# Seven half-size products instead of eight in the first feed-forward net of a decoder layer too, with its right factors made during the first block's downs

## The chip, the core and the metric

The kernel runs on one core of a Trainium2 chip. The metric is the device time of one launch in microseconds; before the change the median of 3 runs is 1263.14 us (1262.64 to 1269.46). TensorE is called PE, VectorE DVE, ScalarE ACT, GpSimd POOL and SyncE SP, as in the profile.

## What is computed

One inference step of a decoder layer over 544 tokens (512 of a prompt, 8 x 4 new ones of samples with a paged cache), width 1024, hidden width 2816, all in float32. Cut to what matters here:

```
def swiglu(x, w_gate, w_up, w_down):
    return (jax.nn.silu(x @ w_gate) * (x @ w_up)) @ w_down

x = x + 0.5 * swiglu(rmsnorm(x, ffn1_norm), ffn1_w_gate, ffn1_w_up, ffn1_w_down)
h = rmsnorm(x, mix_norm)           # mixer: gated convolution and sparse attention
x = x + concat(y_conv, attn) @ w_out
x = x + 0.5 * swiglu(rmsnorm(x, ffn2_norm), ffn2_w_gate, ffn2_w_up, ffn2_w_down)
```

## The kernel before

**Layout.** The 544 tokens lie along the free dimension, in two halves of 272; the 1024 channels are 8 chunks `c` of 128 partitions, the 2816 features 22 tiles `f` of 128. Each float32 operand is split into a high part (ACT copies it to float32r) and a low part (DVE subtracts), and each product is three matmuls: high by high, high by low, low by high. The weights' parts are `whi` and `wlo` (line 169 and 174, tiles of 128x1024, three slots of each), those of the activations `xh` and `xl`, those of the hidden layer `hh` and `hl`.

**A feed-forward net** runs in blocks of features, `BLOCKS` (line 27), of 8, 8 and 6. For each feature tile of a block the gate `G` and the up `U` are made (48 matmuls of 272 columns each in the plain form, `wmm`, line 194), scaled by the tokens' norm `R`, passed through Silu and multiplied. Then come the downs: for each of the 8 chunks one product `Y` of the block's hidden tiles, which DVE adds to `x` with factor one half. PSUM has eight banks: two places of two banks (`wunit`, tag w), two of one bank (`funit`, tag f), and one each of `sunit` and `tunit`.

**The first net** (`ffn`, line 266) has the plain form throughout. Its beginning (`begin_units`) makes feature 0 while the input still comes in; after the last block each chunk of `x` is squared and split for the mixer (`done1`).

**The second net** (`ffn_late`, line 449) makes features 0 to 3 in the plain form and then two features at once by seven half-size products for eight (Winograd's form of Strassen's). `right` (line 382) makes seven right factors, sums and differences of the quarters of the scaled `x`, kept in `x3h`, `x3l` and in the places of `xh`, `xl`. `factors` (line 343) makes the seven left ones of two weight tiles: POOL makes four sums and differences (`s12`, `s34`, line 367), ACT and DVE their parts (lines 359 and 360). `unit` (line 418) runs the products, each 12 matmuls of 272 columns, 84 in all, and puts them together: ACT copies products 0 and 1 out of PSUM (`m1`, `m5`, lines 436 and 437), DVE adds the others (lines 439 to 447). Products 2 and 4 have the two halves of one two-bank place, products 5 and 6 those of another.

**What sets the order.** A scheduler with a model of the times places each engine's instructions; each engine then runs its own in that order and waits for semaphores. A new tile in a place waits until all readers of the old one are done, and a write into a tile waits for earlier reads of that tile, also of another part of it. Weights come over SP's queue through three buffers `wst` (a fourth, `wst4`, in the second net). POOL's queue also issues the gathers of the cache.

Of the kernel before, what the change touches and what calls it, by code (L numbers as in the profile page):

```python
# [26 lines left out]
BLOCKS = [(0, 8), (8, 16), (16, 22)]  # L27
# [31 lines left out]
SB = 1  # L59
ZB = 1  # L60
# [60 lines left out]
class Trunk:  # L121
# [144 lines left out]
    def ffn(self, wg, wu, wd, done, late=False):  # L266
        nc = self.nc
        wdv = wd.rearrange("(f p) n -> p f n", p=128)

        def hidden(f, G, U):  # L270

            t, s, u = (fp.tile([128, T], F32, name=n, tag=n, bufs=2) for n in ("t", "ts", "u"))

            def scale(dst, src):
                if isinstance(src, list):
                    for cs, p in src:
                        nc.vector.tensor_mul(dst[:, cs], p, self.R[:, cs])  # L277
                else:
                    nc.vector.tensor_mul(dst.rearrange("p (a b) -> p a b", a=2), src[:, :, :HT], self.R.rearrange("p (a b) -> p a b", a=2))  # L279
            scale(t, G)  # L280
            nc.scalar.activation(s, t, AF.Silu)
            scale(u, U)
            nc.vector.tensor_mul(u, u, s)
            nc.scalar.activation(hh[:, f - f0, :], u, AF.Copy)
            nc.vector.tensor_sub(hl[:, f - f0, :], u, hh[:, f - f0, :].bitcast(F32))

        with self.tc.tile_pool(name="ffn", bufs=1) as fp:
            for f0, f1 in BLOCKS:
                nf = f1 - f0
                hh = fp.tile([128, 8, T], F32R, name="hh", tag="hh", bufs=1)  # L290
                hl = fp.tile([128, 8, T], F32R, name="hl", tag="hl", bufs=1)
                for f in range(f0, f1):
                    act = self.xh, self.xl
                    if f == 0 and not late:
                        first = self.begin_units()
                        continue
                    gp = self.cols(wg, f * 128, 128)
                    if f == 1:
                        self.spread()
                        G = list(self.fmm("G", gp, act, KC))  # L300
                        hidden(0, *first)
                    else:
                        G = self.wunit("G")
                        self.wmm(G, gp, act)
                    if f == 0:
                        self.rms_from_S()
                    U = self.wunit("U")
                    self.wmm(U, self.cols(wu, f * 128, 128), act)
                    if f == 0:
                        first = G, U  # L310
                    else:
                        hidden(f, G, U)
                    if f == 2 and not late:
                        self.begin_rest()
                end = f1 == BLOCKS[-1][1]
                for c in range(KC):
                    parts = self.stream(lambda stv: [(stv, wdv[:, f0:f1, c * 128:(c + 1) * 128])], nf, 128)
                    if end and c == KC - 1:
                        for i, (c0, c1) in enumerate(TILES):
                            Y = self.wunit("Y")  # L320
                            self.wmm(Y, parts, (hh, hl), TILES, (i,))
                            if late and i == 0:
                                done(c - 1)
                            xc = self.x[:, c, c0:c1]
                            nc.vector.scalar_tensor_tensor(xc, Y[:, i, :c1 - c0], 0.5, xc, op0=ALU.mult, op1=ALU.add)
                            done(c, i)
                    else:
                        Y = self.wunit("Y")
                        self.wmm(Y, parts, (hh, hl))
                        if end and late and c:  # L330
                            done(c - 1)
                        xc = self.x[:, c, :].rearrange("p (a b) -> p a b", a=2)
                        nc.vector.scalar_tensor_tensor(xc, Y[:, :, :HT], 0.5, xc, op0=ALU.mult, op1=ALU.add)  # L333
                        if end and not late:
                            done(c)

# [36 lines left out]
    def right(self, scale, place, nk):  # L373
# [6 lines left out]
        for k0 in range(0, n, nk):  # L380
            v = fp.tile([128, 2, nk, 2, HT], F32, name="xn", tag=place, bufs=1)
            both = [slice(k, k + 2) for k in range(0, nk, 2)]
            (b11, b12), (b21, b22) = [[v[:, r, :, c] for c in range(2)] for r in range(2)]

            def row(r):
                for k in range(nk):
                    c, dst = r * n + k0 + k, v[:, r, k].rearrange("p c n -> p (c n)")
                    if r == 0:
                        V.scalar_tensor_tensor(dst, self.x[:, c, :], scale[:, c:c + 1], self.R, op0=ALU.mult, op1=ALU.mult)
                    else:  # L390
# [1332 lines left out]
```

## Time and profile before

| | |
|---|---|
| median of 3 runs (lowest, highest) | 1263.14 us (1262.64, 1269.46) |
| the profiled execution's own time | 1267.7 us |
| its span, first to last instruction | 1265.9 us |
| PE busy | 1213.1 us, 96% |
| DVE, ACT, POOL busy | 752.9, 504.0, 347.4 us (59, 40, 27%) |
| mean granted clock of PE | 0.991 of full speed |
| chain of work that ended last, by engine | PE 77%, DVE 15%, issue 3%, DMA 2% |
| the three largest lines of that chain | PE Y L194 20%, PE U L194 11%, PE G L194 10% |

The shares are means over stages with different limits. By the chain and the stage table below, the first net takes the span to 412.3 us, the mixer to about 869 us, and the second net the rest. L194 is the plain form, L433 the seven products, L133 and L137 are the mixer's matmuls and transposes.

### The profile page before, as it was taken

The page shows a single profiled execution, that of the slowest core. Times are in us where ns is not written, and L with a number is a line of the kernel's source. Part 1 is how long each engine was busy: PE and PEld are TensorE (multiplying, and loading weights), DVE is VectorE, ACT ScalarE, POOL GpSimd, SP SyncE. Part 2 cuts the span into 40 slices and gives each one's busy share as a digit, 9 for nine tenths or more (in the row PEclk, how much of TensorE's full clock was granted, in tenths as well). Part 3 has the DMA queues.
Part 4 walks back from the last instruction along what each step waited for, and adds up shares of the span by engine and source line. Part 5 has one row for each costly group of instructions (what it writes and reads, how often), then busy time and mean ns, then how long its engine had stood idle before and what let it go on. Part 6 is the DMA issues. An engine that isn't in the chain of part 4 may idle for free.

```text
span 1265.9 us, 22810 instructions
## 1 busy us (share of the span) xinstructions
PE 1213.1 (96%) x9413; PEld 1093.1 (86%) x9413; DVE 752.9 (59%) x1332; ACT 504.0 (40%) x769; POOL 347.4 (27%) x401
## 2 busy tenths in 40 slices
PE   9999999999999999899988989989989999999998
PEld 8999999999999746776667545779989999999998
DVE  5444334433446216999998853236997469845972
ACT  6322122211324464456534545435544144423432
POOL 3200000000000555665422322321661255305500
PEclk9999999999999998999998999999999999999999
DMA  7432233233222554145222644444314312332322
GB/s 230 127 93 84 84 93 91 84 92 93 84 68 76 163 178 122 51 142 170 68 65 92 201 151 134 155 135 121 91 51 117 114 54 84 112 106 67 96 79 80
DMA packets 184363, 136.09 MB, mean 108 GB/s; under 512 B 5706, under 2 KB 172434, under 8 KB 184260
## 3 DMA queue, kind: packets, MB, share of 16 engines
q1 hardware_dynamic: 171700, 91.62, 24.9%
q0 software_dynamic: 11904, 42.26, 10.4%
q8 instruction: 74, 1.21, 0.4%
q10 hardware_dynamic: 656, 0.76, 0.2%
q14 instruction: 29, 0.24, 0.1%
HBM read 131.66 MB, written 2.96 MB: 106 GB/s over the span
## 4 chain that ended last, share of the span: by engine, by line
PE 77%; DVE 15%; issue 3%; DMA 2%; ACT 1%; POOL 1%; DVEq 0%; ACTq 0%; POOLq 0%
PE Y L194 20%; PE U L194 11%; PE G L194 10%; PE U L433 7%; PE G L433 5%; PE Yo L133 4%; DVE flip L1034 3%; PE KTp L137 2%; PE lg L133 2%; PE nat L133 2%; PE O L133 1%; DMA ckn<-in_cache_k,ik 1%; PE ssc L133 1%; PE gc L133 1%; PE plg L133 1%
## 5 line engine op out<-in xcount | busy, mean ns | idle before, releaser
L169 ACT ACTIVATE whi<-wst 128x1024 fp32r<-128x1024 f32 (+3 forms) x137 | 134.0, 982 | 377.6 <-PE Y L194 123.9
L174 DVE TENSOR_TENSOR wlo<-wst,whi 128x1024 fp32r<-128x1024 f32 (+3 forms) x120 | 138.7, 1156 | 23.8 <-ACT whi L169 21.2
L172 POOL TENSOR_TENSOR wlo<-wst,whi 128x1024 fp32r<-128x1024 f32 (+2 forms) x17 | 34.4, 2022 | 423.8 <-ACT whi L169 423.3
L194 PE MATMUL Y<-hh,whi 128*128 128x272 f32 (+2 forms) x704 | 147.8, 289 | 0.0
L194 PE MATMUL Y<-hh,wlo 128*128 128x272 f32 (+2 forms) x704 | 147.1, 288 | 0.0
L194 PE MATMUL Y<-hl,whi 128*128 128x272 f32 (+2 forms) x704 | 147.0, 288 | 0.0
L194 PEld LDWEIGHTS Y<-hl,whi 128*128 128x128 f32 x704 | 111.3, 189 | 0.0
L194 PEld LDWEIGHTS Y<-hh,whi 128*128 128x128 f32 x704 | 111.0, 188 | 0.0
L194 PEld LDWEIGHTS Y<-hh,wlo 128*128 128x128 f32 x704 | 110.8, 188 | 0.0
L367 POOL TENSOR_TENSOR s<-wst 128x512 f32<-128x512 f32 x36 | 55.6, 1547 | 169.9 <-DMA wst<-in_ffn_w_gate 90.8
L194 PE MATMUL U<-xh,whi 128*128 128x272 f32 x336 | 69.4, 287 | 1.8 <-DVE t L277 1.8
L194 PE MATMUL U<-xh,wlo 128*128 128x272 f32 x336 | 69.1, 288 | 0.0
L194 PE MATMUL U<-xl,whi 128*128 128x272 f32 x336 | 69.0, 287 | 0.0
L194 PE MATMUL G<-xh,whi 128*128 128x272 f32 x320 | 66.1, 288 | 0.0
L194 PE MATMUL G<-xh,wlo 128*128 128x272 f32 x320 | 65.8, 288 | 0.0
L194 PE MATMUL G<-xl,whi 128*128 128x272 f32 x320 | 65.7, 287 | 0.0
L279 DVE TENSOR_TENSOR u<-U,R 128x544 f32<-128x544 f32 x21 | 15.2, 725 | 79.4 <-PE U L194 79.4
L360 DVE TENSOR_TENSOR wlo<-s,whi 128x1024 fp32r<-128x1024 f32 x36 | 55.6, 1544 | 5.9 <-ACT whi L359 5.9
L333 DVE SCALAR_TENSOR_TENSOR x<-Y,x 128x544 f32<-128x544 f32 x23 | 16.7, 725 | 70.8 <-PE Y L194 70.8
L537 DVE SCALAR_TENSOR_TENSOR x<-Y,x 128x544 f32<-128x544 f32 x23 | 16.6, 723 | 65.1 <-PE Y L194 65.1
L194 PEld LDWEIGHTS U<-xh,whi 128*128 128x128 f32 x336 | 52.3, 188 | 2.0 <-ACT whi L169 2.0
L359 ACT ACTIVATE whi<-s 128x1024 fp32r<-128x1024 f32 x36 | 38.0, 1056 | 37.9 <-PE Y L194 19.8
(422 smaller groups left out, 3501.3 us busy)
## 6 DMA issues: line engine op xcount, KB each, us to landing
wst<-in_ffn_w_up SPq DMA_DIRECT2D x44, 512.0 KB, 3.7
wst<-in_ffn_w_gate SPq DMA_DIRECT2D x43, 512.0 KB, 3.6
wst<-in_ffn_w_down SPq DMA_DIRECT2D x32, 512.0 KB, 4.0
wst<-in_w_in SPq DMA_DIRECT2D x16, 512.0 KB, 4.0
wst<-in_ffn_w_down SPq DMA_DIRECT2D x16, 384.0 KB, 3.5
xn<-in_x_prompt SPq DMA_DIRECT2D x4, 512.0 KB
wst<-in_w_in SPq DMA_DIRECT2D x8, 256.0 KB, 7.9
wst<-in_w_out SPq DMA_DIRECT2D x8, 256.0 KB, 2.8
```

The costliest lines, as they stand in the source:

```text
L133: ins = self.nc.tensor.matmul(*args, **kw)
L137: ins = self.nc.tensor.transpose(*args)
L169: nc.scalar.activation(hi, st, AF.Copy)
L172: nc.gpsimd.tensor_tensor(lo, st, hi.bitcast(F32), op=ALU.subtract)
L174: nc.vector.tensor_sub(lo, st, hi.bitcast(F32))
L194: self.nc.tensor.matmul(unit[:, i, :c1 - c0], a[:, k, :], b[:, k, c0:c1], start=k == 0 and j == 0, stop=k == n - 1 and j == 2)
L333: nc.vector.scalar_tensor_tensor(xc, Y[:, :, :HT], 0.5, xc, op0=ALU.mult, op1=ALU.add)
L359: nc.scalar.activation(hi, src, AF.Copy)
L360: nc.vector.tensor_sub(lo, src, hi.bitcast(F32))
L367: nc.gpsimd.tensor_tensor(dst, a, b, op=op)
L433: nc.tensor.matmul(out, w[:, k, :], b[:, k, :], start=k == 0 and j == 0, stop=k == nk - 1 and j == 2)
L1034: V.tensor_scalar(junk, src, cand[:, k:k + 1], None, op0=ALU.is_ge, op1=ALU.add, accum_out=cnt[:, k:k + 1])
```

## The change

The old `ffn` goes, and `ffn_late` becomes `ffn` for both nets. In the first net the blocks are now features 0 to 5, 6 to 13 and 14 to 21. The first block keeps the plain form (its hidden parts are now made for two features at once, `parts_of`); the other two have the seven products. The right factors of the first net are made while the first block's downs run: `right` is now a generator in steps, of which two are taken ahead of each chunk, the chunks come in the order 0, 1, 4, 5, 2, 3, 6, 7, so that no chunk of `x` is updated before it has been read, and with `alone` set POOL has no part in them: DVE scales all eight chunks and makes the differences. In the second net `right` is taken at one go, with POOL, as before. In `unit` product 2 has the place `sunit` and product 4 one of the two `funit`, in both nets; only products 5 and 6 share a two-bank place. At the start the input tiles lie in places that the first net uses later.

```diff
-BLOCKS = [(0, 8), (8, 16), (16, 22)]
+BLOCKS = [[(0, 6), (6, 14), (14, 22)], [(0, 8), (8, 16), (16, 22)]]
+RSTEPS = 2
...
-    def ffn(self, wg, wu, wd, done, late=False):
...
+    def parts_of(self, u, k, hh, hl):
+        if hh is None:
+            hh, hl = (self.fp.tile([128, 8, T], F32R, name=n, tag=n, bufs=1) for n in ("hh", "hl"))
+        self.nc.scalar.activation(hh[:, k:k + 2], u, AF.Copy)
+        self.nc.vector.tensor_sub(hl[:, k:k + 2], u, hh[:, k:k + 2].bitcast(F32))
+        return hh, hl
...
-    def right(self, scale, place, nk):
+    def right(self, scale, place):
...
-                    if r == 0:
+                    if r == 0 or self.alone:
                         V.scalar_tensor_tensor(dst, self.x[:, c, :], scale[:, c:c + 1], self.R, op0=ALU.mult, op1=ALU.mult)
                     else:
                         nc.scalar.activation(dst, self.x[:, c, :], AF.Copy, scale=scale[:, c:c + 1])
...
+                hi, lo = (a[:, j, k0:k0 + 2] for a in t)
+                nc.scalar.activation(hi, src, AF.Copy)
+                V.tensor_sub(lo, src, hi.bitcast(F32))
+            less = (V if self.alone else P).tensor_tensor
             row(0)
             split(0, b11)
+            yield
             row(1)
+            yield
+            less(t3, b22, b12, op=ALU.subtract)
+            V.tensor_sub(b12, b12, b11)
             split(1, b12)
+            yield
+            less(b11, b22, b12, op=ALU.subtract)
             split(2, b11)
+            yield
             split(3, b21)
+            yield
             split(4, t3)
+            yield
+            less(b21, b21, b11, op=ALU.subtract)
             split(5, b22)
+            yield
             split(6, b21)
+            yield
...
         nc.scalar.activation(m1, product(0, self.funit(name)[:, :HT]), AF.Copy)
         nc.scalar.activation(m5, product(1, self.funit(name)[:, :HT]), AF.Copy)
-        w = self.wunit(name)
-        V.tensor_add(z[:, 0], product(2, w[:, 0, :HT]), m1)
+        V.tensor_add(z[:, 0], product(2, self.sunit(name)[:, :HT]), m1)
         p = product(3, self.tunit(name)[:, :HT])
         V.tensor_add(z[:, 3], p, m1)
-        V.tensor_add(z[:, 2], product(4, w[:, 1, :HT]), z[:, 0])
+        V.tensor_add(z[:, 2], product(4, self.funit(name)[:, :HT]), z[:, 0])
...
-    def ffn_late(self, wg, wu, wd, done):
+    def ffn(self, wg, wu, wd, scale, done, late=False):
...
+        def shared(k0):
+            s, u = quarters("s"), quarters("u")
+            return [t[:, 0:4].rearrange("p (k c) n -> p k c n", k=2) for t in (s, u)], s[:, 4:6]
...
+            if f0 == 0 and not late:
+                rest = self.right(scale, shared)
+            for c in (0, 1, 4, 5, 2, 3, 6, 7) if f0 == 0 else range(KC):
+                if f0 == 0:
+                    for _ in range(RSTEPS):
+                        next(rest, None)
+                if c == KC - 1:
+                    list(rest)
                 parts = self.stream(lambda stv: [(stv, wdv[:, f0:f1, c * 128:(c + 1) * 128])], nf, 128)
...
-            xn = [ip.tile([128, D], F32, name=f"xn{t}") for t in range(5)]
+            xn = [xin[:, t] for t in range(4)] + [xin2[:, 0]]
```

Where the scheduler now puts things, at three places. In the first block's downs of the first net, DVE before, from the last up of the block on (`wlo` is the low part of the next weights):

```order
L279 TENSOR_TENSOR u<-U,R 128x544
L283 TENSOR_TENSOR u<-u,ts 128x544
L174 TENSOR_TENSOR wlo<-wst,whi 128x1024
L285 TENSOR_TENSOR hl<-u,hh 128x544
L333 SCALAR_TENSOR_TENSOR x<-Y,x 128x544
L174 TENSOR_TENSOR wlo<-wst,whi 128x1024
L333 SCALAR_TENSOR_TENSOR x<-Y,x 128x544
```

and DVE now, from the second addition on (`s` and `u` hold the scaled quarters; L336 are the factors' low parts, L349 and L356 differences):

```order
L509 SCALAR_TENSOR_TENSOR x<-Y,x 128x544
L336 TENSOR_TENSOR xl<-u,xh 128x544 x2
L336 TENSOR_TENSOR xl<-s,xh 128x544
L349 TENSOR_TENSOR s<-u,s 128x2x272
L175 TENSOR_TENSOR wlo<-wst,whi 128x768
L336 TENSOR_TENSOR x3l<-s,x3h 128x544
L509 SCALAR_TENSOR_TENSOR x<-Y,x 128x544
L356 TENSOR_TENSOR u<-u,s 128x2x272
L175 TENSOR_TENSOR wlo<-wst,whi 128x768
L336 TENSOR_TENSOR x3l<-s,x3h 128x544
L336 TENSOR_TENSOR xl<-u,xh 128x544
L509 SCALAR_TENSOR_TENSOR x<-Y,x 128x544
```

Between two additions, where one weight part stood, there are now three to five instructions more. In the first net, POOL before, from the gathers' addresses on:

```order
L724 TENSOR_SCALAR ik<-pbase 128x8 x4
L900 DMA kn<-in_cache_idx_k,ii 128x1024 x2
L172 TENSOR_TENSOR wlo<-wst,whi 128x984
L1523 MEMSET qbd 128x256
L900 DMA kn<-in_cache_idx_k,ii 128x1024 x3
```

and POOL now, the first of 64 sums and differences of the weights (`s` with its number, four to a unit):

```order
L700 TENSOR_SCALAR ik<-pbase 128x8 x4
L876 DMA kn<-in_cache_idx_k,ii 128x1024 x2
L297 TENSOR_TENSOR s_1408<-wst 128x512
L297 TENSOR_TENSOR s_1409<-wst 128x512
L297 TENSOR_TENSOR s_1408<-s_1408,wst 128x512
L297 TENSOR_TENSOR s_1409<-wst,s_1408 128x512
```

All 64 stand between the second gather and the weight part `wlo` of 128x984; three memsets that stood at the program's start now follow that part. In a late pair of the second net, DVE before, in a gate unit (`m` with its number is the copied product 0 or 1):

```order
L439 TENSOR_TENSOR s<-G,m_11380 128x272
L519 TENSOR_TENSOR hl<-u,hh 128x1088
L441 TENSOR_TENSOR s<-G,m_11380 128x272
L360 TENSOR_TENSOR wlo<-s_11487,whi 128x1024
L360 TENSOR_TENSOR wlo<-wst,whi 128x1024
L442 TENSOR_TENSOR s<-G,s 128x272
L443 TENSOR_TENSOR s<-s,m_11381 128x2x272
L360 TENSOR_TENSOR wlo<-s_11488,whi 128x1024
L447 TENSOR_TENSOR s<-G,s 128x544
```

and DVE now, in such a unit of the second net, to its last addition:

```order
L377 TENSOR_TENSOR s<-G,m_11568 128x272
L484 TENSOR_TENSOR hl<-u,hh 128x1088
L290 TENSOR_TENSOR wlo<-s_11676,whi 128x1024
L379 TENSOR_TENSOR s<-G,m_11568 128x272
L290 TENSOR_TENSOR wlo<-wst,whi 128x1024
L380 TENSOR_TENSOR s<-G,s 128x272
L381 TENSOR_TENSOR s<-s,m_11569 128x2x272
L290 TENSOR_TENSOR wlo<-s_11677,whi 128x1024
L385 TENSOR_TENSOR s<-G,s 128x544
```

The same instructions follow each other; a weight part has moved ahead of the addition of product 3 (L441, now L379).

## Rows read from the trace of the kernel before

**Rows 1.** stretches: us; busy PE, PEld, DVE, ACT, POOL; clock, DMA share, GB/s

```profile
88.85:112.75 23.90, 23.90 (x195) 23.90 (x194) 10.34 (x12) 6.69 (x9) 0.00 (x0) 1.00 0.30 89
112.75:160.85 48.10, 48.10 (x386) 48.10 (x386) 16.88 (x18) 9.20 (x10) 0.00 (x0) 1.00 0.30 89
...
376.21:412.30 36.09, 36.09 (x289) 35.89 (x287) 24.04 (x31) 16.52 (x23) 2.32 (x1) 1.00 0.24 72
412.30:869.10 456.80, 422.12 (x3130) 307.64 (x3130) 298.27 (x801) 228.92 (x409) 186.71 (x286) 0.97 0.42 131
...
971.80:1019.83 48.03, 48.03 (x387) 48.03 (x386) 19.67 (x21) 9.33 (x11) 9.09 (x6) 1.00 0.35 102
1019.83:1107.77 87.94, 85.24 (x674) 84.43 (x674) 76.34 (x81) 42.31 (x55) 42.79 (x26) 1.00 0.31 89
```

**Rows 2.** chain of waits in order of time: start, us, what

```profile
340.37 5.97 PE G L194 x48
...
1030.37 10.52 PE U L433 x84
...
1073.99 6.14 PE U L433 x48
```

**Rows 3.** PE's waits, 950 to 1266 us: total us, times, longest

```profile
PE G L433 <- DVE s L439: 3.9, 3, 1.3
```

**Rows 4.** timeline of PE: start, us, what, idle before and releaser

```profile
1061.76 0.29 PE L433 MATMUL G<-x3h,whi 128*128 128x272 f32 x1
...
1070.72 0.39 PE L433 MATMUL G<-xh,whi 128*128 128x272 f32 x1 [1.28 <-DVE s L439]
```

**Rows 5.** timeline of DVE, one pair of the second net

```profile
1070.22 0.44 DVE L439 TENSOR_TENSOR s<-G,m 128x272 f32<-128x272 f32 x1
1071.27 1.29 DVE L519 TENSOR_TENSOR hl<-u,hh 128x1088 fp32r<-128x1088 f32 x1 [0.60 <-ACT hh L518]
...
1072.83 1.22 DVE L360 TENSOR_TENSOR wlo<-s,whi 128x1024 fp32r<-128x1024 f32 x1
1073.96 1.22 DVE L360 TENSOR_TENSOR wlo<-wst,whi 128x1024 fp32r<-128x1024 f32 x1
...
1076.83 2.31 DVE L360 TENSOR_TENSOR wlo<-s,whi 128x1024 fp32r<-128x1024 f32 x1
1079.06 0.71 DVE L447 TENSOR_TENSOR s<-G,s 128x544 f32<-128x544 f32 x1
...
1081.23 0.44 DVE L439 TENSOR_TENSOR u<-U,m 128x272 f32<-128x272 f32 x1 [0.18 <-ACT m L436]
1082.47 1.23 DVE L360 TENSOR_TENSOR wlo<-s,whi 128x1024 fp32r<-128x1024 f32 x1 [0.79 <-ACT whi L359]
...
1093.36 0.44 DVE L439 TENSOR_TENSOR s<-G,m 128x272 f32<-128x272 f32 x1
```

**Rows 6.** DVE by line and form, 100 to 376 us: busy us, mean ns

```profile
L333 DVE SCALAR_TENSOR_TENSOR x<-Y,x 128x544 f32<-128x544 f32 x16 | 11.6, 725 | 60.4 <-PE Y L194 60.4
...
L285 DVE TENSOR_TENSOR hl<-u,hh 128x544 fp32r<-128x544 f32 x15 | 10.8, 719 | 0.7 <-ACT hh L284 0.7
L174 DVE TENSOR_TENSOR wlo<-wst,whi 128x768 fp32r<-128x768 f32 x2 | 1.9, 959 | 0.0
```

**Rows 7.** DVE by line and form, 860 to 1221 us

```profile
L211 DVE SCALAR_TENSOR_TENSOR hl<-x,par,hh 128x544 fp32r<-128x544 f32 x6 | 4.7, 777 | 0.0
```

**Rows 8.** timeline of ACT in that pair

```profile
1079.81 1.12 ACT L480 ACTIVATE s<-s 128x1088 f32<-128x1088 f32 x1 [5.20 <-DVE s L447]
1080.83 0.38 ACT L436 ACTIVATE m<-U 128x272 f32<-128x272 f32 x1
```

**Rows 9.** timeline of POOL

```profile
0.99 0.53 POOL L1537 MEMSET qbi<- 128x512 f32 x1
...
414.07 1.07 POOL L900 DMA_INDIRECT kn<-in_cache_idx_k,ii  x1 [1.39 <-PE KTp L137]
...
1016.12 1.29 POOL L367 TENSOR_TENSOR s<-wst 128x512 f32<-128x512 f32 x1 [7.60 <-issue]
```

## What was predicted before the change was timed

> **What bounds the kernel now.** I read the busy time stage by stage first, then the chain of waits, then what TensorE (PE) waits for, then the DVE, ScalarE (ACT) and GpSimd (POOL) instructions of one stretch in which PE does wait. In the first FFN, PE is busy without a gap at a granted clock of 1.00 (the 2.4 GHz level): the gates and ups of two feature tiles take 23.90 us, the eight downs of a block 48.10 us, those of the last, shorter block 36.09 us [rows 1]. DVE is there at 10.34 of 23.90 us and POOL at zero. So this stage ends when PE ends, and fewer matmuls in it are worth their full time as long as the others keep up. The second FFN already works with seven products: 84 matmuls of 10.52 us where two tiles of the plain form need 2 x 48 in 2 x 5.97 us [rows 2]. There PE is not quite full: its block of four pairs takes 87.94 us with DVE at 76.34 and POOL at 42.79 [rows 1], and PE waits three times about 1.3 us for the DVE instruction L439 [rows 3]. The mixer between them (456.80 us, PE 422.12 busy) has the same work in both kernels.
>
> The place of that wait: the gate product began at 1061.76, ran 60 matmuls and stood until 1070.72, when L439 had emptied the third product (product 2 of `unit`) [rows 4]. L439 is late because DVE is: from one L439 to the next of the same kind are 23.14 us (1070.22 to 1093.36) for 21 instructions, with about 1.6 us of idle time (0.60, 0.18 and 0.79, each for ACT) [rows 5]. A pair costs DVE and ACT together 23.14 us, PE only 2 x 10.52 = 21.04. In the first two pairs PE is ahead because DVE had caught up during the downs (19.67 of 48.03 us busy there [rows 1]); then it waits.
>
> **PE.** Eight pairs of the first FFN (features 6 to 21) go from 4 x 5.97 = 23.88 to 21.04 us: 8 x 2.84 = 22.7 us off. The downs stay: 8 x 22 x 6 matmuls as before, cut 6, 8, 8 instead of 8, 8, 6, so 36.09 + 48.10 + 48.10 us in another order.
>
> **Making the right factors, during the first block's downs.** It adds to DVE eight scalings and 22 plain ones of 128x544 (eight differences, fourteen low parts): 8 x 0.78 + 22 x 0.72 = 22.1 us by [rows 6, 7]. Beside them stand what the downs need (8 additions of 0.725, six weight parts of 0.96, about 2 us of the block's last hidden part: 13.6 us) and the low parts of the first seven-product unit (three of 1.22 and one half as wide, 4.3 us). Sum 40.0 us; back-to-back rows start some 0.08 us before the one ahead ends (1072.83 + 1.22 against 1073.96 [rows 5]), which takes about 4 off over 50 instructions: 36 us of DVE in 36.09 us of PE. The last of it, the fourth weight part, is wanted only six microseconds into the next stage. PE needs from DVE here the addition that frees its PSUM place, and the order puts each addition behind at most five of the new instructions (3.6 us), under the 4.5 us that a chunk of downs takes PE. ACT gets fourteen high parts, each shorter than the 1.12 us of a Silu twice as wide [rows 8]: under 16 us beside its 9.20 of 48.10. So I charge PE 0.5 us here; the bounds are 0 and 6 (all four units beyond 36, plus two collisions with POOL of 1.1 us each, below). POOL is not given the work, and the hidden parts of the first six features, now written two at a time, lie under PE as before.
>
> **The two blocks with seven products.** Now DVE and POOL do here what they do in the second FFN. The block of features 14 to 21 begins, like that one's, after 48 us of downs with DVE free, so it should take nearly its 87.94 us. The block of 6 to 13 begins with DVE late by the right factors: its first evictions come perhaps 2 us later than after quiet downs, and PE is held from the first or second pair on; I take 89.2. Together 176.6 instead of 191.2 us (8 x 23.9). Bounds: 8 x 21.04 = 168.3 (PE never waits) and 8 x 23.14 = 185.1 (DVE's pace throughout).
>
> **Own PSUM places.** The third product no longer shares a two-bank tile with the fifth (product 4), so the fifth needn't wait for L439. It takes a place of the two that the first two products use instead, and so waits for ACT to have copied the first product away (m). On ACT that copy stands behind the Silu of the gate, and the Silu behind DVE's last gate addition: L447 at 1079.06, Silu 1079.81, copy at 1080.83 to 1081.21 [rows 5, 8]. In the up product the fifth is due 48 matmuls, 6.0 us, after its start at 1073.99 [rows 2], at 1080.0: 1.2 us too early. Behind the held matmul on PE stand the last three products (36 matmuls, 4.5 us), and for them wait the additions of DVE. The hold of 1.3 us leaves the gate and one of 1.2 us enters the up. As DVE's and ACT's 23.14 us per pair do not change, little can come of it. I take 1 us off for the second FFN's nine pairs, with bounds of 3.9 off (all three waits of [rows 3] go) and 3 on.
>
> **Nothing else.** The 64 instructions on POOL stand between its second and third gather; before, the third and later gathers also began only after the first FFN, and the zeroing of three more tiles that now stands ahead of them (the longest 0.53 us) falls into the 1.39 us for which the third waits for PE's transposes [rows 9]. SyncE loads the same weights in a slightly other order; the DMA share of this stage is 0.30 [rows 1]. The mixer's order on DVE shifts by a few places: 0, with bounds of 4 either way.
>
> **Sum.** From 88.85 (the seventh tile's start) to 412.30 the profile has 323.45 us. After: 36.1 + 0.5 + 89.2 + 48.1 + 87.4 + 48.1 = 309.4, so 14.0 off; with the 1 of the second FFN 15. The profiled execution took 1267.7 us (span 1265.9) and becomes 1252.7; the median of the runs is 1263.14, 4.6 lower, and becomes 1248.
>
> **Rivals.**
> Nothing waits: DVE and ACT follow PE in both FFNs. Then 22.7 + 3.9 - 0.5 = 26 us go: 1237. For it: the fifth product's wait comes from a shared tile alone, and in the first two pairs of each block PE ran free. Against: 23.14 us per pair on DVE. By the Trainium skill (PSUM — Partial Sum Buffer, Summary: rules for kernel authors) PSUM is to be guarded by bank, and a matmul may write one bank while another is read; the two halves of the old tile are two banks, so by this rule the old wait protects nothing, and its removal is pure gain. The trace shows no run without it.
> DVE sets the pace from the first pair and also during the factors: 8 x (23.9 - 23.14) = 6.1 off, 4 lost in the downs: 1261, no change.
> Slower: each of the eight POOL instructions per pair holds DVE for its whole length. DVE's same part takes 1.22 us alone and 2.31 beside POOL [rows 5], 1.09 more, near one POOL instruction of 1.29 [rows 9]; the stretched ones among the 21 make 5.6 us, some five such holds. With three more in each pair, 23.14 + 3 x 1.09 = 26.4 us, over the 23.9 of the plain form from which it decides: 8 x 2.5 = 20 us lost, and 2 to 4 in the downs: 1286. Against: the second FFN runs the same eight beside the same DVE work at 23.14. The Trainium skill (SBUF — State Buffer, Who interferes with whom) says that a DVE instruction with two SBUF inputs and a GpSimd instruction that reads SBUF exclude each other for a whole instruction; the trace agrees (2.31 for 1.22). That rule speaks against putting POOL to work in a stage where it had none.
> The mixer's shifted order costs 5 us or more: about 1254.
>
> **Chances.** The forecast 0.65 (own range 1243 to 1253), nothing waits 0.12, DVE's pace 0.08, mixer 0.12, POOL's holds 0.03. A measurement of this kernel can tell 0.5%, 6.3 us, from no change: under 1256.8 lie the forecast, the free case and most of the mixer's case, 0.89; no change 0.08; slower 0.03. The range of 8 in 10 is 1240 to 1257: it takes in part of the free case and of the mixer's.
>
> **What would show it.** Right: a gate and an up of 84 matmuls in 10.5 us from about 125 us on; first downs of about 36.5 us; blocks of 88 to 90 and 87 to 88 us with POOL at some 43; PE's waits in a seven-product unit on the ACT copy of m in the up, none on the eviction of the third product in the gate; the first FFN ending near 398. Wrong: pairs above 23 us from the start, downs of over 40 us with PE waiting for the addition of x, a second FFN more than 4 us off its 397 us, or a mixer more than 4 us from 456.8.

## The result, and the profile after

The changed kernel takes 1255.26 us (median of 5 runs, 1253.65 to 1256.43) against 1265.08 us (5 runs, 1262.64 to 1269.46) of the kernel before on the same chip: a ratio of 0.9915, with a 95% interval of 0.9888 to 0.9942. A second time (e12 below) it was 0.9911 (0.9890 to 0.9932). So 10 to 12 us went by the medians, where 15 had been predicted, and the interval leaves 7 to 14. 1255.26 lies in the range of 1240 to 1257, but above the forecast's own 1243 to 1253. The profiled execution took 1253.65 us.

The page has PE at 95% as before, DVE at 69% instead of 59%, POOL at 36% instead of 27%:

```profile
PE 1192.6 (95%) x9216; PEld 1070.5 (86%) x9221; DVE 858.7 (69%) x1433; ACT 544.2 (43%) x830; POOL 446.3 (36%) x465
...
PE 67%; DVE 22%; issue 5%; DMA 3%; ACT 2%; POOL 1%; DVEq 0%; ACTq 0%; POOLq 0%
```

In the chain DVE has risen from 15 to 22%, PE fallen from 77 to 67%: the end now hangs on DVE in more places. The stages of the changed kernel (columns as in [rows 1]: first downs, features 6 to 13, features 14 to 21, mixer, second FFN; the downs of the two later blocks, 48.19 and 48.26 us, are left out):

```profile
88.06:124.18 36.12, 36.12 (x291) 36.12 (x290) 35.98 (x46) 16.11 (x23) 9.04 (x4) 1.00 0.32 93
124.18:214.21 90.03, 87.02 (x674) 86.06 (x674) 82.71 (x85) 42.55 (x56) 46.16 (x28) 0.98 0.32 94
...
262.40:351.21 88.81, 86.58 (x674) 85.91 (x674) 77.71 (x81) 42.55 (x55) 40.47 (x26) 0.98 0.29 84
...
399.47:854.12 454.65, 419.04 (x3124) 304.27 (x3128) 294.42 (x802) 228.20 (x407) 187.56 (x289) 0.98 0.43 131
854.12:1251.90 397.78, 384.48 (x3032) 380.72 (x3030) 276.80 (x301) 151.21 (x199) 134.61 (x83) 0.99 0.30 88
```

The first FFN from its first downs on takes 399.47 - 88.06 = 311.41 us instead of 323.45 [rows 1]: 12.0 off. The mixer is 2.15 shorter, the second FFN 1.0 longer than its 1265.9 - 869.10 = 396.8 before. In the first downs DVE has 35.98 us in 36.12 and PE does not wait.

What PE waits for in the seven products is no longer the eviction of [rows 3]; it is now the low part of the weights (`wlo`, L290), in the up. From 60 to 440 us (us in total, times, longest):

```profile
PE U L372 <- DVE wlo L290: 5.0, 4, 1.6
...
PE U L372 <- ACT m L375: 0.2, 1, 0.2
```

and from 840 to 1260 us, in the second net:

```profile
PE U L372 <- DVE wlo L290: 6.3, 7, 2.0
```

The window of [rows 3] began at 950 us and left out the second net's first pairs. Over all of that net, 840 to 1260 us, the kernel before has:

```profile
PE G L433 <- DVE s L439: 5.1, 4, 1.3
PE G L433 <- DVE wlo L360: 1.4, 1, 1.4
...
PE U L433 <- DVE wlo L360: 1.2, 1, 1.2
```

The last line is the wait that the changed kernel has seven times: the kernel before had it once already. A wait for `wlo` in a gate, 1.4 us, stands in both; with it the waits in the second net's seven products add up to 7.7 us before and 7.7 us after. They have changed place and not become less.

One of these waits, on PE, DVE, ACT and POOL (start, us, what; idle time before and its releaser in brackets):

```profile
180.06 0.29 PE L372 MATMUL U<-x3h,whi 128*128 128x272 f32 x1
181.95 0.39 PE L372 MATMUL U<-x3h,wlo 128*128 128x272 f32 x1 [1.60 <-DVE wlo L290]
```

```profile
176.97 1.29 DVE L484 TENSOR_TENSOR hl<-u,hh 128x1088 fp32r<-128x1088 f32 x1 [0.61 <-ACT hh L483]
178.18 1.22 DVE L290 TENSOR_TENSOR wlo<-s,whi 128x1024 fp32r<-128x1024 f32 x1
179.31 0.44 DVE L379 TENSOR_TENSOR s<-G,m 128x272 f32<-128x272 f32 x1
179.66 2.23 DVE L290 TENSOR_TENSOR wlo<-wst,whi 128x1024 fp32r<-128x1024 f32 x1
```

```profile
175.82 1.12 ACT L483 ACTIVATE hh<-u 128x1088 fp32r<-128x1088 f32 x1 [3.69 <-DVE u L421]
...
177.79 1.04 ACT L289 ACTIVATE whi<-wst 128x1024 fp32r<-128x1024 f32 x1
```

```profile
179.53 1.28 POOL L297 TENSOR_TENSOR s<-wst 128x512 f32<-128x512 f32 x1 [4.33 <-DVE wlo L290]
180.90 2.15 POOL L297 TENSOR_TENSOR s<-s,wst 128x512 f32<-128x512 f32 x1
```

Read backwards: PE has begun the up and stands until the low part of its first weight tile is there (179.66 to 181.89). That row takes 2.23 us instead of the 1.22 of the one above it, because POOL's sum began beside it; POOL had waited for the `wlo` of 178.18 to let go of its tile. And the row is late, because ACT stood idle 3.69 us for the hidden part `hh` of the pair before and made the weights' high parts only behind it.

### The profile page after: what moved, and what is told of

It is laid out like the page before. It is cut to its first block, busy times and chain, and to the rows that moved or that the text cites. A ratio compares the mean times of both kernels' runs of the same rounds, so it can differ in the third digit from the quotient of the medians.

```text
span 1251.9 us, 22739 instructions
## 1 busy us (share of the span) xinstructions
PE 1192.6 (95%) x9216; PEld 1070.5 (86%) x9221; DVE 858.7 (69%) x1433; ACT 544.2 (43%) x830; POOL 446.3 (36%) x465
## 4 chain that ended last, share of the span: by engine, by line
PE 67%; DVE 22%; issue 5%; DMA 3%; ACT 2%; POOL 1%; DVEq 0%; ACTq 0%; POOLq 0%
PE Y L195 21%; PE U L372 10%; PE G L372 6%; DVE wlo L290 5%; PE Yo L134 3%; PE lg L134 3%; PE U L195 3%; PE nat L134 3%; PE KTp L138 3%; PE G L195 2%; DVE flip L1010 2%; DMA ckn<-in_cache_k,ik 1%; PE ssc L134 1%; DVE u L421 1%; PE O L134 1%
## 5 line engine op out<-in xcount | busy, mean ns | idle before, releaser
L297 POOL TENSOR_TENSOR s<-wst 128x512 f32<-128x512 f32 x68 | 98.2, 1448 | 363.7 <-DMA wst<-in_ffn_w_gate 209.0
L170 ACT ACTIVATE whi<-wst 128x1024 fp32r<-128x1024 f32 (+3 forms) x105 | 99.9, 957 | 203.9 <-PE Y L195 72.5
L175 DVE TENSOR_TENSOR wlo<-wst,whi 128x1024 fp32r<-128x1024 f32 (+3 forms) x88 | 99.8, 1134 | 21.3 <-ACT whi L170 19.7
L290 DVE TENSOR_TENSOR wlo<-wst,whi 128x1024 fp32r<-128x1024 f32 (+1 forms) x68 | 96.3, 1416 | 15.4 <-ACT whi L289 15.0
L289 ACT ACTIVATE whi<-s 128x1024 fp32r<-128x1024 f32 x68 | 71.8, 1056 | 70.9 <-PE Y L195 29.8
L290 DVE TENSOR_TENSOR wlo<-s,whi 128x1024 fp32r<-128x1024 f32 x68 | 87.8, 1292 | 10.5 <-ACT whi L289 10.5
L372 PE MATMUL G<-xh,wlo 128*128 128x272 f32 x272 | 78.4, 288 | 0.0
L372 PE MATMUL G<-xl,whi 128*128 128x272 f32 x272 | 78.1, 287 | 0.0
L289 ACT ACTIVATE whi<-wst 128x1024 fp32r<-128x1024 f32 (+1 forms) x68 | 57.2, 841 | 42.4 <-DMA wst<-in_ffn_w_gate 17.3
L372 PE MATMUL U<-x3h,wlo 128*128 128x272 f32 x204 | 61.4, 306 | 11.3 <-DVE wlo L290 11.3
```

Source lines behind the costliest of these rows:

```text
L170: nc.scalar.activation(hi, st, AF.Copy)
L175: nc.vector.tensor_sub(lo, st, hi.bitcast(F32))
L289: nc.scalar.activation(hi, src, AF.Copy)
L290: nc.vector.tensor_sub(lo, src, hi.bitcast(F32))
L297: nc.gpsimd.tensor_tensor(dst, a, b, op=op)
L372: nc.tensor.matmul(out, w[:, k, :], b[:, k, :], start=k == 0 and j == 0, stop=k == nk - 1 and j == 2)
```

## The experiments

The stages of all runs in us, each from one profiled execution of that kernel (what stands there in the kernel before: [rows 1]; there, and in e2, the first column is the same point, the end of feature 5); the last column is the median of all its executions:

| kernel | first downs begin | they take | features 6-13 | 14-21 | mixer | second FFN | median |
|---|---|---|---|---|---|---|---|
| before | 88.85 | - | - | - | 456.8 | 396.8 | 1265 to 1267 |
| changed | 88.06 | 36.12 | 90.03 | 88.81 | 454.7 | 397.8 | 1255.26 |
| e12 changed, again | 86.75 | 36.12 | 89.82 | 88.46 | 455.9 | 397.7 | 1254.18 |
| e1 shared place | 86.93 | 36.12 | 88.72 | 87.93 | 459.1 | 396.8 | 1253.62 |
| e2 before, own places | 90.09 | - | - | - | 454.0 | 398.4 | 1267.37 |
| e3 no sums | 86.95 | 36.12 | 84.22 | 84.22 | 456 | 386.3 | 1232.93 |
| e4 hidden later | 86.93 | 36.12 | 87.95 | 85.36 | 456.3 | 392.4 | 1245.55 |
| e5 later, shared place | 86.92 | 36.12 | 90.70 | 89.10 | 455.8 | 397.8 | 1255.88 |
| e6 fewer factors | 87.96 | 36.14 | 86.44 | 85.61 | 455.9 | 394.7 | 1243.27 |
| e7 more factors | 86.65 | (132.1 together) | | 85.34 | 456.4 | 392.0 | 1251.11 |
| e8 POOL makes factors | 88.03 | 44.78 | 86.24 | 85.38 | 456.1 | 392.0 | 1251.62 |
| e9 s12 on DVE | 88.09 | 36.12 | 84.52 | 84.18 | 454.2 | 388.6 | 1234.87 |
| e10 s34 on DVE | 86.92 | 36.12 | 84.46 | 84.16 | 454.2 | 388.6 | 1232.43 |
| e11 all sums on DVE | 86.68 | 36.12 | 84.32 | 84.16 | 456.4 | 387.9 | 1232.92 |

The mixer's work is the same in all of them and took 454.0 to 459.1 us; the two kernels with the old first net have 454.0 and 456.8. So its 2.15 us in the changed kernel cannot be told from what it varies by, and medians a few us apart are read by stages.

The first column holds something that the prediction did not count. In the executions with a wait of PE of some 2 us at 10 us from the start, the first downs begin at 87.96 to 88.09 us with the new beginning (the changed kernel, e6, e8, e9) and the same point is reached at 90.09 with the old one (e2). In those without it they begin at 86.65 to 86.95 with the new one and it is reached at 88.85 with the old one. So like for like the new beginning is some 2 us shorter. The page of the kernel before has a wait that none of the twelve executions with the new beginning has (the last number; it stands at 34.47 us, and e2 has it too, 1.92 us at 35.70):

```profile
L194 PE MATMUL U<-xh,whi 128*128 128x272 f32 x336 | 69.4, 287 | 1.8 <-DVE t L277 1.8
```

Why it went no run separates.

**e1_shared_place.** Own places undone in both FFNs:

```diff
-        V.tensor_add(z[:, 0], product(2, self.sunit(name)[:, :HT]), m1)
+        w = self.wunit(name)
+        V.tensor_add(z[:, 0], product(2, w[:, 0, :HT]), m1)
...
-        V.tensor_add(z[:, 2], product(4, self.funit(name)[:, :HT]), z[:, 0])
+        V.tensor_add(z[:, 2], product(4, w[:, 1, :HT]), z[:, 0])
```

> The changed kernel with one part undone in both FFNs: products 2 and 4 of a unit have the two halves of one two-bank place again. Theory A (a pair is paced by DVE and ACT, the own places only move PE's wait from the eviction of product 2 to the weights' low part, where it is longer and brings the clock down): PE waits 1.2 to 1.4 us for that eviction, no stretch near those waits below a clock of 0.95, blocks 6-13 and 14-21 at 88 to 89 and 87.5 to 88.5 us (90.03 and 88.81 with own places), second FFN 396 to 397 us (397.8): 3 to 5 us faster than the changed kernel, about 1250. Theory B (own places are a gain, as predicted): waits come on top of those for the low part, blocks 90 to 92, second FFN 398 to 400, 2 to 5 us slower than the changed kernel, about 1258.

1253.62 us, ratio to the kernel before 0.9903 (0.9887 to 0.9920): by time not to be told from the changed kernel, since the intervals overlap. By stages it is theory A: PE's waits are back at the eviction of product 2 (the first net),

```profile
PE G L372 <- DVE s L378: 5.2, 4, 1.4
```

the two blocks are 0.5 to 1.3 us shorter each than in the two executions of the changed kernel, the second FFN 1.0 shorter. Features 6 to 13, e1 and then the changed kernel in e12, both at a clock of 1.00:

```profile
123.05:211.77 88.72, 85.94 (x674) 84.67 (x674) 81.87 (x85) 42.31 (x56) 47.41 (x28) 1.00 0.32 94
```

```profile
122.87:212.69 89.82, 86.12 (x674) 84.70 (x674) 82.64 (x85) 42.17 (x56) 45.52 (x28) 1.00 0.32 93
```

The 1250 of theory A did not come. In the profiled execution the mixer's 459.1 us took back what the stages gave; for the other three executions the stages are not known. The edit also changes the order that the scheduler gives DVE. In the changed kernel a low part stands ahead of the addition of product 3 (178.18 and 179.31 above), and the next one, for which PE waits, meets POOL's sum and takes 2.23 us. In e1 the addition comes first (176.47), both low parts behind it take their 1.21 and 1.22 us (176.82, 177.96), and the stretched one is a later one (2.31 us at 180.83). What the places do by themselves and what this order does the runs do not separate.

**e2_places_alone.** The same edit the other way round, in the kernel before.

> The kernel before with one part of the change alone: product 2 in the one-bank place of its own and product 4 in one of the two others, in the second FFN, which alone has seven products there. Theory A: second FFN 396.5 to 398.5 us (before 396.8), time within 0.2% of the kernel before, waits for the weights' low part of 1.5 to 2 us. Theory B: second FFN 393 to 396 us, 1 to 4 us faster than before. Its first FFN is that of the kernel before, so it also shows whether the mixer's 454.65 us after the change (456.8 before) is the change's or lies within what the mixer varies by between executions: in the second case its mixer is anywhere between 454 and 458.

1267.37 us, ratio 1.0009 (0.9996 to 1.0022). The second FFN takes 398.43 instead of 396.80 us, with the waits of the changed kernel (840 to 1260 us):

```profile
PE U L433 <- DVE wlo L360: 6.3, 7, 2.0
```

So own places alone are worth nothing, and by the stage of this one execution lose 1.6 us: theory A.

**e3_no_sums.** POOL's four sums of a unit left out; p1 and p2 take the quarters of the second tile, p3 and p4 those of the first.

```diff
...
-            nc.gpsimd.tensor_tensor(dst, a, b, op=op)
-        p1, p2 = parts(s12, 2)
-        p3, p4 = parts(s34, 2)
+        p1, p2 = parts(st[1], 2)
+        p3, p4 = parts(st[0], 2)
```

> The changed kernel without POOL's four sums and differences of the weights in a unit: the products that want them take the plain quarters, so the values differ and nothing else does. Theory A (POOL's 8 instructions per pair stretch DVE's, and their place in the chain from one low part to the next makes the pair 23.2 us): the pair falls to PE's own 21.0 to 21.4 us, blocks 84 to 86 us each, second FFN 390 to 393, time 1236 to 1242. Theory C (the pace is the count of DVE and ACT instructions and their order, POOL costs little): blocks 87.5 to 89.5, time 1250 to 1254.

1232.93 us, 22 less than the changed kernel, more than theory A gave (1236). In the two blocks PE runs without a gap:

```profile
123.07:207.29 84.22, 84.22 (x674) 84.22 (x674) 61.90 (x83) 44.18 (x55) 0.00 (x0) 1.00 0.37 104
255.49:339.71 84.22, 84.22 (x674) 84.22 (x674) 61.32 (x82) 43.72 (x55) 0.00 (x0) 1.00 0.33 96
```

The same DVE instructions (82 against 81) are busy 61.32 us here and 77.71 in the changed kernel's block 14-21: POOL's 26 sums cost DVE 16.4 us, 0.63 each.

**e4_hidden_later.** In each pair the hidden parts of the pair before (`held`) are queued on ACT and on DVE behind the parts of the up's first weight tile (`self.after` holds those two instructions):

```diff
+            left = cols(wu, f)
+            act, dve = self.after
+            with self.tc.issue_after(act.ins), self.tc.issue_after(dve.ins):
+                held()
...
             nc.scalar.activation(s[:, 3:7], s[:, 3:7], AF.Silu)
-            self.unit("U", cols(wu, f), xs, KC // 2, u)
+            self.unit("U", left, xs, KC // 2, u)
```

> The changed kernel with the hidden layer's high and low part of the pair before (hh on ACT, hl on DVE) queued behind the high and low part of the up's first weight tile; nothing else is changed by hand. Theory A1 (PE's wait in the up comes from this order: ACT stands idle 3.7 us until hh and makes the weights' high parts only then): the waits of 1.2 to 2.0 us for the low part go, the clock stays at 1.00, pairs of 21.2 to 22.3 us, blocks 85 to 87.5 us, second FFN 393 to 396, time 1242 to 1248. Theory A2 (DVE's 21 instructions, stretched by POOL, are the floor whatever their order): the pair stays at 22.8 to 23.4, the wait comes elsewhere, blocks 88 to 90, time 1251 to 1256.

1245.55 us, ratio 0.9843 (0.9829 to 0.9857): 9.7 less than the changed kernel (some 9 by the ratios), without one instruction less. Theory A1, in time and in the second block; the first block's 87.95 lies just above it, the second FFN's 392.4 just below. ACT now makes the weights' parts first:

```profile
150.67 1.06 ACT L289 ACTIVATE whi<-wst 128x1024 fp32r<-128x1024 f32 x1 [0.41 <-PE G L372]
151.64 1.10 ACT L491 ACTIVATE hh<-u 128x1088 fp32r<-128x1088 f32 x1
```

and of 5.0 us of waits for `wlo` in the ups of the first FFN 2.3 are left, none above 1.0 (L289 is the line of `wlo` here). In the second FFN 3.6 of 6.3 are left; its longest wait, 2.0 us in the first of that net's pairs, has stayed.

**e5_later_shared.** e4 with the edit of e1.

> The version with the hidden parts queued later (e4_hidden_later), with products 2 and 4 in one shared two-bank place again. Theory A (the place decides only where a late DVE holds PE; with DVE earlier there is nothing to hold): first FFN and second FFN within 1 us of e4_hidden_later's (blocks 87.95 and 85.36, second FFN 392.4), time 1244.5 to 1246.5. Theory B (own places are worth something of their own once no drop of the clock follows): 2 to 5 us slower than e4_hidden_later, with waits of PE for the eviction of product 2.

1255.88 us, ratio 0.9918 (0.9890 to 0.9946): ten us slower than e4, which neither theory had. The later order gains only with own places. With two tiles of the two-bank places per unit the up's fifth product on PE (48 matmuls stand before it) waits for the gate's last addition (L386), so it takes, as I read it, the tile that this addition must first empty:

```profile
162.60 0.37 PE L372 MATMUL U<-xh,whi 128*128 128x272 f32 x1 [0.92 <-DVE s L386]
168.66 0.40 PE L372 MATMUL G<-x3h,wlo 128*128 128x272 f32 x1 [0.82 <-DVE wlo L289]
```

So the places do take a constraint away; in the order that the changed kernel has, another wait stands right behind it.

**e6_fewer_factors, e7_more_factors.** On e4: the 14 low parts of the first FFN's right factors left out (the high parts stand for them), or made twice.

```diff
-                V.tensor_sub(lo, src, hi.bitcast(F32))
+                if not self.alone:
+                    V.tensor_sub(lo, src, hi.bitcast(F32))
```

```diff
-                V.tensor_sub(lo, src, hi.bitcast(F32))
+                for _ in range(2 if self.alone else 1):
+                    V.tensor_sub(lo, src, hi.bitcast(F32))
```

> The version e4_hidden_later, with the 14 low parts of the first FFN's right factors left out (the high part stands in for each, so the values differ): 14 x 0.72 = 10 us of DVE less during the first block's downs. Theory D (DVE just fits under those downs and comes out of them late, which is why block 6-13 takes 2.6 us more than block 14-21): the downs stay at 36.1, block 6-13 falls from 87.95 to 85.3 to 86.3, the rest as before, time 1243 to 1244.5. Theory E (block 6-13 is longer for another reason, as the phase in which POOL's sums meet DVE): it stays within 0.7 us of 87.95.

> The version e4_hidden_later, with each of those 14 low parts made twice: 10 us of DVE more. Theory D (DVE full at 35.98 of 36.12 us): all of it comes out at the end, in PE's waits for the addition of x or in the block behind: downs and block 6-13 together 132 to 135 us where e4_hidden_later has 124.1, time 1253 to 1256. Theory F (there is slack: the overlaps of rows and the idle places of the block behind take most of it): 125 to 128 us, time 1246 to 1249.

1243.27 and 1251.11 us. Ten us more of DVE (e7) make downs and first block 132.08 us instead of 36.12 + 87.95 = 124.07: 8.0 come out at the end, as theory D had it by stages; the time lies between the two theories. DVE was full there: it is busy for all of the first 10.00 us behind the downs. Some of the 8.0 can be the clock's, which stood at 0.50 from 131.50 to 138.30 us in this execution. Ten less (e6) leave the downs as they were, with DVE at 27.77 us, and take 1.5 us off block 6-13: 86.44, just above what theory D gave. It is still 0.8 us longer than block 14-21, where e4 had 2.6, for another reason:

```profile
87.96:124.10 36.14, 36.14 (x291) 36.14 (x290) 27.77 (x35) 16.91 (x25) 8.66 (x6) 1.00 0.37 106
124.10:210.54 86.44, 84.95 (x674) 84.51 (x674) 77.93 (x81) 43.14 (x55) 42.04 (x27) 1.00 0.31 91
```

**e8_pool_factors.** On e4: `self.alone` false, so POOL and ACT take part in the factors.

```diff
-        self.alone = not late
+        self.alone = False
```

> The version e4_hidden_later, with POOL and ACT taking part in the first FFN's right factors as in the second's (POOL four multiplications and the three differences per half that the second net gives it). DVE loses four scalings and six differences, some 7.5 us, and its other instructions are stretched beside POOL's. Theory G (POOL's instructions hold DVE's two-input ones for most of their own length, 14 of them of 1.3 to 2.5 us): no gain, downs of 36.1 to 38, block 6-13 of 87.5 to 90, time 1245 to 1249. Theory H (POOL's help relieves DVE): block 6-13 falls to 85.3 to 86.5, time 1243 to 1244.5.

1251.62 us: the downs take 44.78 us instead of 36.12, worse than G had; PE stands 5.2 us for the addition of x, since six rows of DVE lie between that one and the one before it, and all but one of them are stretched beside POOL (128x544 takes 0.71 us above them):

```profile
107.03 0.71 DVE L336 TENSOR_TENSOR xl<-u,xh 128x544 fp32r<-128x544 f32 x1
...
114.72 0.71 DVE L520 SCALAR_TENSOR_TENSOR x<-Y,x 128x544 f32<-128x544 f32 x1
115.36 1.54 DVE L336 TENSOR_TENSOR xl<-u,xh 128x544 fp32r<-128x544 f32 x1
116.82 1.81 DVE L346 TENSOR_TENSOR s<-s 128x544 f32<-128x544 f32 x1
118.55 0.94 DVE L175 TENSOR_TENSOR wlo<-wst,whi 128x768 fp32r<-128x768 f32 x1
119.42 1.88 DVE L336 TENSOR_TENSOR xl<-s,xh 128x544 fp32r<-128x544 f32 x1
121.22 1.75 DVE L289 TENSOR_TENSOR wlo<-wst,whi 128x512 fp32r<-128x512 f32 x1
122.89 1.85 DVE L336 TENSOR_TENSOR x3l<-s,x3h 128x544 fp32r<-128x544 f32 x1
124.66 0.71 DVE L520 SCALAR_TENSOR_TENSOR x<-Y,x 128x544 f32<-128x544 f32 x1
```

From 124.15 to 132.81, where that wait ends, PE's granted clock is 0.61 on the mean. Block 6-13 falls to 86.24, as H had it, but that gives back 1.7 of 8.7. Leaving POOL out here was worth 7 us by stages, 4 to 6 by ratio and median.

**e9_s12_on_dve, e10_s34_on_dve, e11_sums_on_dve.** On e4: two or all four of a unit's sums made by DVE; `eng` is DVE for s12, for s34, or for all, and POOL for the rest:

```diff
-            nc.gpsimd.tensor_tensor(dst, a, b, op=op)
+            eng.tensor_tensor(dst, a, b, op=op)
```

> The version e4_hidden_later, with POOL's first two sums of a unit (s12) made by DVE instead. Per block of four pairs DVE gets 16 more of some 0.65 us (10 us) and loses about half of what POOL's instructions stretch (76.9 to 83.3 us of DVE with them in e4_hidden_later, 61.9 without in e3_no_sums: 15 to 21 us, half 8 to 10). Theory I (a sum costs DVE about the same, made or suffered): DVE's busy time stays, blocks within 1 us of 87.95 and 85.36, time 1244 to 1247. Theory J (POOL's latency, 1.29 and 1.74 us in a row ahead of ACT and DVE, holds the chain too): blocks 84.5 to 86, time 1240 to 1243.

> The same with POOL's other two sums of a unit (s34) made by DVE. Theory I: within 1 us per block of e4_hidden_later, 1244 to 1247. Theory J: these come later in the chain and free POOL for s12 earlier, blocks 84.5 to 86, 1240 to 1243.

> The same with all four sums of a unit made by DVE, none by POOL. DVE then has some 62 + 32 x 0.65 = 83 us in a block, where PE has 84.2. Theory I: no row of DVE is stretched, the block ends when DVE does, 84.5 to 87 us each, second FFN 389 to 393, time 1240 to 1245. Theory K (DVE without slack is late with evictions, and PE waits for them): blocks 87 to 91, time 1247 to 1256.

1234.87, 1232.43 and 1232.92 us; ratios 0.9762 (0.9736 to 0.9788), 0.9751 (0.9722 to 0.9781), 0.9740 (0.9714 to 0.9765). All three are faster than any theory had said, and e10 and e11, with the full computation, as fast as e3, which leaves the sums out. Block 14-21, e10 and then e11:

```profile
255.70:339.86 84.16, 84.16 (x674) 84.16 (x674) 78.57 (x96) 43.58 (x55) 21.91 (x12) 1.00 0.31 89
```

```profile
255.31:339.47 84.16, 84.16 (x675) 84.16 (x674) 75.22 (x107) 43.47 (x55) 0.00 (x0) 1.00 0.30 87
```

In this block PE no longer waits. In e11 DVE has 26 instructions more than in the changed kernel's block and is busy 75.22 us instead of 77.71: a sum adds (75.22 - 61.32) / 26 = 0.53 us to DVE where DVE makes it, and 0.63 where POOL does. Of DVE's rows by form, features 6 to 13, the changed kernel first and then e11 (busy us, mean ns):

```profile
L290 DVE TENSOR_TENSOR wlo<-wst,whi 128x512 fp32r<-128x512 f32 x7 | 8.7, 1236 | 0.0
L381 DVE TENSOR_TENSOR s<-s,m 128x544 f32<-128x544 f32 x4 | 4.8, 1191 | 0.1
...
L385 DVE TENSOR_TENSOR s<-G,s 128x544 f32<-128x544 f32 x4 | 2.9, 714 | 0.0
```

```profile
L297 DVE TENSOR_TENSOR s<-wst 128x512 f32<-128x512 f32 x14 | 9.6, 684 | 0.0
...
L289 DVE TENSOR_TENSOR wlo<-wst,whi 128x512 fp32r<-128x512 f32 x7 | 4.8, 684 | 0.0
...
L381 DVE TENSOR_TENSOR s<-s,m 128x544 f32<-128x544 f32 x4 | 2.9, 719 | 0.0
L385 DVE TENSOR_TENSOR s<-G,s 128x544 f32<-128x544 f32 x4 | 2.9, 718 | 0.0
```

Only the rows with both inputs in SBUF are stretched beside POOL (1191 for 719 ns, 1236 for 684); the addition that reads the product `G` from PSUM is not (714, 718). By the Trainium skill (SBUF — State Buffer, Who interferes with whom) a DVE instruction with at most one SBUF input, outside the two-port modes, does not contend with GpSimd, and one with two contends with a GpSimd instruction that reads SBUF; the trace agrees in both halves.

**e12_after_again.** The changed kernel itself.

> The changed kernel itself once more, beside the others on one chip. If the falls of the clock in its blocks come with certain waits each time, blocks of 90.0 and 88.8 us and a second FFN of 397.8 return; if they fall differently from one execution to the next, a block without one takes 88.0 to 88.4 (the first) or 86.9 to 87.2 (the second). The mixer shows what it varies by: 454.65 us in the execution profiled first, 454 to 459 in the other kernels, which have the same mixer. Time 1253 to 1257.

1254.18 us, ratio 0.9911 (0.9890 to 0.9932). PE waits at the same places, and in the seven products the clock stayed at 1.00 this time. Behind the wait at 181.95 in the first profiled execution, and behind its counterpart in this one (us; PE busy; granted clock, DMA share, GB/s):

```profile
181.95:183.95 2.00, 2.00 (x10) 0.61 0.35 99
183.95:185.95 2.00, 2.00 (x11) 0.54 0.55 164
```

```profile
180.64:184.64 4.00, 4.00 (x32) 1.00 0.44 131
```

The blocks are nevertheless only 0.2 and 0.35 us shorter; the expectation of 88.0 to 88.4 and 86.9 to 87.2 without a fall of the clock was wrong, and so was the reading of the first profile behind it, that the two falls had cost 3.5 us together. Where DVE sets the pace, PE at half speed only waits less afterwards: in the first FFN 5.0 us of waits with the falls, 6.2 without.

## Why the prediction was right, and where it was off

**PE's saving** held: units of 84 matmuls take 10.52 us, and where nothing holds PE (e3, e11) a block of four pairs takes 84.2, the 4 x 21.04 of the prediction's lower bound.

**The right factors** held: 36.12 us with DVE at 35.98, so the charge of 0.5 was not needed. e7 shows that there was no slack (8.0 of 10 us come out, some of it perhaps by the clock), e6 that DVE's lateness is more than half of why the first block is longer, e8 that POOL's help would have cost 8.7 us of downs.

**The two blocks** came at 89.8 to 90.0 and 88.5 to 88.8 us for 89.2 and 87.4: 2 us more together. The pace in the held pairs, from the end of one hold in an up to the end of the next, is 181.95 - 158.68 = 23.27 us, the 23.14 of [rows 5] and a little more (rows of the chain of waits):

```profile
158.68 4.88 PE U L372 x37
...
181.95 11.19 PE U L372 x75
```

**Own PSUM places** is the step that failed. It said: 1 us off the second FFN, the hold moving from the eviction to ACT's copy of m in the up. It cost 1.0 (397.8 and 397.7 for 396.8), and the copy holds PE for 0.2 us once. I had looked only for who must release the place, and not for who else would be late when PE comes 1.3 us earlier to the next unit: the low part of its first weights. The trace of the kernel before had that wait once, at 940.47 us, outside the window of [rows 3]. PE now stands there instead, for 0.6 or 1.6 us in most pairs, and DVE's rows meet POOL's a little worse (82.71 and 82.64 us of DVE in block 6-13, 81.87 in e1). Without own places the blocks take 88.72 + 87.93 = 176.65 us (e1), the 176.6 of the forecast, though there two errors of 0.5 us cancel (89.2 and 87.4). So the 2 us of the blocks and the 2 of the second FFN look like one mistake. This rests on the stages of one execution of e1 and two of the changed kernel; the medians alone do not show it. The Trainium skill (PSUM — Partial Sum Buffer, Summary: rules for kernel authors) guards PSUM by bank, and by it the old wait protected nothing; no run speaks against that, but by e2 (1.0009) taking away a wait which protects nothing gained nothing either.

**The mixer** at nothing: held, within what it varies by.

**The sum.** With own places at their measured price the 15 us off become 11. The medians have 9.8 and 11.8, but that agreement is partly luck: the beginning, put at nothing, gave some 2 us more. The profiled executions differ by 14.05 us, of which 12.0 are the first FFN's from its first downs on, 0.8 the beginning's (2.1 against e12), 2.15 the mixer's and -1.0 the second FFN's. The profiled execution of the kernel before stood 1.7 to 2.6 us above its medians (1265.08 and 1265.99), as the prediction said of its 1267.7, that of the changed kernel 1.6 below its own; in which stages the other executions differ is not on record. The median before had been taken at 1263.14, from three executions; with 1265.08 the same 15 us give 1250 and not 1248. So of the 7 us by which 1255.26 exceeds 1248, 2 lie in that base.

**The rivals.** "Nothing waits" (1237) did not come true for this kernel, but e4 and e10 show that it was the nearer limit than I thought: DVE's 23.14 us per pair, on which the forecast rests, is no floor. It contains POOL's stretches and ACT's order. In e10 DVE is busy 81.26 of 84.46 us and PE hardly waits, in the changed kernel 82.71 of 90.03. The mixer's rival named about 1254, which is the time that came, but the mixer took 454.65 and 455.87 us for 456.80: the number met and the mechanism did not. "DVE's pace from the start" fell with the pairs that ran at 21.04; the POOL rival had the right mechanism at the wrong place: the holds were already in the 23.14. How the gain of e9 to e11 divides between rows that are not stretched and POOL's two sums in a row no longer standing ahead of ACT and DVE is not separated by these runs.

The best version is e10 or e11, some 22 us under the changed kernel and 33 under the one before (e10 1232.43, e11 1232.92 beside 1265.99 on the same chip).

## What to carry to other kernels

When a wait goes, look one unit ahead for the operand that will be late instead; a freed place shows its worth only together with the order that can use it (e1 has neither; own places alone and the later hidden parts alone gained nothing, both together 8 us, e4 beside e1). Before taking an engine's time per round as a floor, see how much of it are rows stretched beside another engine: work handed to POOL can cost DVE more than doing it itself. And a pace set by DVE hides what PE loses, to the clock too, so price such a loss only where PE sets the pace.

## What the runs showed of the hardware

The granted clock fell behind some of PE's waits and not behind others at the same place of the same program: behind 1.60 us at 181.95 it was 0.61 and 0.54, in the second execution it stayed at 1.00. Where DVE sets the pace a fall cost little: a block with one took 0.2 and 0.35 us more, by one pair of executions, and the changed kernel's second FFN with one (925.06) took 397.78 us beside 397.73 without. In e6, whose order lets DVE come earlier, more of it stayed. Behind a wait of 2.0 us, behind which e4 kept 1.00, the up ran at the 1.2 GHz level,

```profile
919.39:923.39 4.00, 4.00 (x17) 4.00 (x18) 3.96 (x5) 0.53 (x1) 2.20 (x2) 0.50 0.44 131
```

and the rest of it, 78 matmuls, took 12.76 us where e4 has 10.05; the second FFN is 2.4 us longer than e4's (394.7 for 392.4).
